# Low part of the weights first in every block of both mlp layers, and a two-column float32 product in front of each

## The chip, the cores and the metric

The kernel runs on one core of one Trainium2 chip. Its time is the device time of one execution in microseconds; of several executions the median is given. One more execution was taken with the hardware profiler, and all that is said of engines, waits and single instructions comes from that one.

The core's engines have their own instruction streams: PE (TensorE) multiplies matrices, with its weight loads listed apart as PEld; DVE (VectorE) and ACT (ScalarE) do elementwise work; POOL (GpSimd) some more of it; SP (SyncE) issues DMAs. PE writes its results to PSUM, which has eight banks of 512 float32 columns.

## The reference

A trunk of two layers over 256 tokens of width 1024, in float32. Layer 0 mixes tokens with a short gated convolution, layer 1 with a dilated window attention of 8 heads and 3 groups. After the mixer, each layer has a squared-ReLU mlp of width 4096 and a gate on a per-layer input:

```python
h = h + mixed
h = h + squared_relu_mlp(rmsnorm(h, norm_mlp[i]), mlp_w_up[i], mlp_w_down[i])
ple_gate = jax.nn.sigmoid(rmsnorm(h, norm_ple[i]) @ ple_w_gate[i])
h = h + ple_gate * (p[i] @ ple_w_proj[i])
...
def squared_relu_mlp(h, w_up, w_down):
    return jnp.square(jax.nn.relu(h @ w_up)) @ w_down
```

At the end stands one more rmsnorm.

## The kernel before

**Numbers in two parts.** The products run in the type float32r, which is a shortened float32. To keep the precision, each float32 operand is split into a high part, which is the value rounded to float32r, and a low part, which is the rest. A product of x and w is then made of three: high by high, high by low, low by high. Weights come from HBM in slabs of eight 128x128 blocks (`load_to`, on SP's queue). ACT makes the high part of a slab (L356) and DVE the low part (L295, called from `split_to`), up to LOOK slabs ahead of the block that PE works on.

**Blocks.** `block` (from L367) issues PE's work for one 128x128 block of weights. There are three kinds. Kind "n" has three products of 256 columns, one for each of the three partial products (acc_o, acc_C, acc_B, acc_g of layer 0, and the qk of the first head). Kind "w" has two: a short one, low weights by high x, 256 columns into the first half of a PSUM bank, and a long one, high weights by both parts of x side by side, 512 columns into the whole bank. Kind "t" has the weights as the moving operand (acc_v, and acc_g of layer 1). All matmuls of all kinds are issued by L392. "w" serves both mlps (acc_u for the up part, acc_d for the down part), the acc_X of the convolution (key "sc_in"), and the qk of heads 1 to 7 (key "qkv").

**Two halves.** In kind "w", blocks come in pairs: `half` 0 and `half` 1 are two neighbouring column blocks of the weights with the same x, each with a bank of its own. Two lines decide the order of the two products:

```python
products = ((dst[:, 0, :], wlo, x[0][:, k % 2, :]), (flat(dst), whi, flat(x[2][:, k % 2, :, :])))
...
products = products[::-1] if half and key != "qkv" else products
```

So, for every key but "qkv", a pair goes short, long, long, short, and the next pair begins with a short one again. For "qkv" it goes short, long, short, long.

**The order of the work.** `make_plan` writes the whole order of blocks and steps by hand: `begin`, the products of the per-layer input, the convolution, its output projection (acc_o), the mlp of layer 0, the gate, the attention head by head, its output projection (acc_o), the mlp of layer 1, and the last gate with the final norm. `mlp_plan` writes one mlp. It has the up part, 16 pairs of column blocks with 8 blocks each along the width (the first two pairs are interleaved by `head_start`, since x becomes ready bit by bit), then the down part, 4 pairs of column blocks with 32 blocks each. After the fourth pair of the up part stands a step "stat_rows", which has two PE products of its own (ssq, L500). Other steps put float32 products between the blocks: "stat" (ssq, L477: two products of the constant `ones`, two columns each), "scores" (sc, L684), "turn" (transposes, L702) and "values" (o, L723).

**Banks.** `bank` takes one of eight PSUM banks; a block opens its accumulation when its name is first met, and `close` gives it to the step that empties it. The first product of an accumulation has start set and overwrites, all others add. `sums` empties the two banks of a pair: ACT copies the second half of a bank (L411) and DVE adds the first half to it.

Of the kernel before, what the change touches and what calls it, by code (L numbers as in the profile page):

```python
# [219 lines left out]
def width(key):  # L220
    return {"v": GROUPS, "gate1": 4, "proj1": 4}.get(key, 1)
# [32 lines left out]
def tile_trunk(ctx: ExitStack, tc: tile.TileContext, plan, slabs, ap, out):  # L254
    nc = tc.nc
# [7 lines left out]
    def const(shape, name, dtype=F32):  # L263
        return cpool.tile(shape, dtype, tag=name, name=name)
# [15 lines left out]
    def bank(name):  # L280
        return psum.tile([P, 2, S], F32, tag="ps", name=name)
# [9 lines left out]
    def flat(t):  # L291
        return t.rearrange("p i s -> p (i s)")
# [6 lines left out]
    ones = const([P, P], "ones")  # L299
# [8 lines left out]
    acc, left, opened = {}, {}, set()  # L308
    for op in plan:
        if op[0] != "do":  # L310
            key = ((*op[4], op[5]), 0) if op[0] == "w" else (op[4], op[5] if op[0] == "n" else 0)
# [48 lines left out]
    def weights(item):  # L360
        si, at = place[item]
        split_to(si + min(LOOK, 1 + si // 3))
        hi, lo = parts[si]
        n = width(item[0]) * P
        return hi[:, at : at + n], lo[:, at : at + n]

    def block(kind, key, k, col, name, half, operand, m=0, cuts=1):  # L367
        name = (*name, half) if kind == "w" else name
        if name not in opened:
            acc[name] = bank("acc_" + "_".join(map(str, name)))  # L370
        left[name, half if kind == "n" else 0] -= 1
        whi, wlo = weights((key, k, col))
        x = state[operand][k // 2]
        if kind == "n":
            dst = acc[name][:, half, :]
            products = ((dst, wlo, x[0][:, k % 2, :]), (dst, whi, x[1][:, k % 2, :]), (dst, whi, x[0][:, k % 2, :]))

            products = products[::-1] if key == "proj0" else products
        elif kind == "w":

            dst = acc[name]
            products = ((dst[:, 0, :], wlo, x[0][:, k % 2, :]), (flat(dst), whi, flat(x[2][:, k % 2, :, :])))

            products = products[::-1] if half and key != "qkv" else products
        else:
            n = width(key) * P // cuts
            whi, wlo = (t[:, m * n : (m + 1) * n] for t in (whi, wlo))
            dst = flat(acc[name])[:, :n]
            xhi, xlo = (t[:, k % 2, half * P : (half + 1) * P] for t in x[:2])
            products = ((dst, xhi, whi), (dst, xhi, wlo), (dst, xlo, whi))  # L390
        for n, (to, a, b) in enumerate(products):
            nc.tensor.matmul(  # L392
                to,
                a,
                b,
                start=n == 0 and name not in opened,
                stop=n == len(products) - 1 and left[name, half if kind == "n" else 0] == 0,
                skip_group_check=True,
            )
            opened.add(name)  # L400
# [430 lines left out]
    for op in plan:  # L831
        if op[0] != "do":
            block(*op)
        elif op[1] in URGENT:
            with tc.high_priority(offset=HURRY):
                steps[op[1]](*op[2:])
        else:
            steps[op[1]](*op[2:])
# [87 lines left out]
```

## Time and profile before

| what | us |
| --- | --- |
| median of 3 executions | 781.18 |
| lowest and highest of them | 781.16, 781.47 |
| the profiled execution | 780.81 |
| its span, from the first to the last instruction | 779.0 |
| granted TensorE clock, mean over the span | 0.998 of full speed |

The span is shorter than the execution, because starting and ending the program stand outside it. Busy times of the page are unions of the times of single instructions. A matmul's time in a row (395 ns, say) is longer than the distance to the next one, because matmuls overlap in the array; the pace of PE is read from the distances of starts, or from the chain of work, which gives a run of products with its length and its count. In the names, acc_u<-x,wlo is a product with the low part of the weights, acc_u<-x,whi one with the high part. A float32 product shows as two records of PE, a float32r product as one.

### The profile page before, as it was taken

What the parts mean: (1) busy time and instruction counts of PE and PEld (TensorE: products, weight loads), DVE (VectorE), ACT (ScalarE), POOL (GpSimd) and SP (SyncE); (2) the same over time, 40 slices, a digit from 0 to 9 for tenths busy, and PEclk for the clock granted to TensorE, in tenths of its full rate; (3) what the DMA queues carried; (4) which work ended last, traced back from release to release, by engine and by line L of the source; (5) the groups of instructions that cost most, each with busy time, mean ns of one, the idle gap of its engine ahead of it and who ended that gap; (6) DMA issues with size and microseconds to landing.
All of it is one profiled execution on the core that took longest, in us unless ns stands there. A gap on an engine that the chain in (4) does not pass through costs nothing.

```text
span 779.0 us, 12527 instructions
## 1 busy us (share of the span) xinstructions
PE 770.6 (99%) x4856; PEld 701.7 (90%) x4856; DVE 574.6 (74%) x834; ACT 441.4 (57%) x679; POOL 168.0 (22%) x110
## 2 busy tenths in 40 slices
PE   9999999999999999999999999999999999999996
PEld 8999998888888899989989989989988888888885
DVE  6997779898556669888768768767698887555564
ACT  7654565565444446557655655655675555444454
POOL 0000000000000000177867867865000000000002
PEclk9999999999999999999999999999999999999999
DMA  9855555556555554654555455455465556555521
GB/s 319 291 197 189 188 187 183 194 176 201 185 192 185 194 181 142 211 184 153 157 175 163 149 175 164 150 174 190 136 194 188 186 191 190 187 190 191 188 94 55
DMA packets 42539, 140.97 MB, mean 181 GB/s; under 512 B 4848, under 2 KB 6128, under 8 KB 42480
## 3 DMA queue, kind: packets, MB, share of 16 engines
q1 hardware_dynamic: 41904, 139.61, 55.0%
q8 instruction: 38, 0.62, 0.3%
q10 hardware_dynamic: 576, 0.56, 0.2%
q14 instruction: 21, 0.17, 0.1%
HBM read 139.10 MB, written 1.05 MB: 180 GB/s over the span
## 4 chain that ended last, share of the span: by engine, by line
PE 97%; issue 1%; DVE 1%; DMA 0%; POOL 0%; ACT 0%; SPq 0%; POOLq 0%; DVEq 0%
PE acc_u L392 23%; PE acc_d L392 23%; PE acc_qk L392 17%; PE acc_v L392 9%; PE acc_o L392 6%; PE acc_g L392 5%; PE acc_C L392 3%; PE acc_B L392 3%; PE acc_X L392 3%; PE acc_p L392 1%; PE o L723 1%; PE sc L684 1%; PE tp L702 1%; PE sc L681 1%; PE o L717 1%
## 5 line engine op out<-in xcount | busy, mean ns | idle before, releaser
L295 DVE TENSOR_TENSOR wlo<-raw,whi 128x1024 fp32r<-128x1024 f32 (+2 forms) x277 | 350.6, 1272 | 159.2 <-ACT whi L356 157.3
L356 ACT ACTIVATE whi<-raw 128x1024 fp32r<-128x1024 f32 (+2 forms) x277 | 278.4, 1007 | 218.8 <-PE acc_d L392 77.1
L392 PE MATMUL acc_u<-x,whi 128*128 128x512 f32 x512 | 160.8, 395 | 0.0
L392 PE MATMUL acc_d<-u,whi 128*128 128x512 f32 x512 | 160.8, 395 | 0.0
L392 PE MATMUL acc_qk<-x,whi 128*128 128x512 f32 (+1 forms) x432 | 134.5, 368 | 0.0
L462 POOL TENSOR_TENSOR n<-v,power 128x4 f32<-128x4 f32 (+1 forms) x6 | 5.2, 862 | 518.8 <-DVE v L487 514.3
L392 PEld LDWEIGHTS acc_d<-u,wlo 128*128 128x128 f32 x512 | 96.2, 188 | 22.7
L392 PEld LDWEIGHTS acc_u<-x,wlo 128*128 128x128 f32 x512 | 96.2, 188 | 22.6
L392 PE MATMUL acc_qk<-x,wlo 128*128 128x256 f32 x384 | 107.8, 281 | 0.0
L392 PE MATMUL acc_u<-x,wlo 128*128 128x256 f32 x512 | 101.3, 278 | 0.0
L392 PE MATMUL acc_d<-u,wlo 128*128 128x256 f32 x512 | 100.9, 278 | 0.0
L392 PEld LDWEIGHTS acc_qk<-x,whi 128*128 128x128 f32 x432 | 77.9, 188 | 13.7
L651 POOL TENSOR_TENSOR rot<-qk,sinr 16x512 f32<-16x512 f32 x44 | 78.3, 1780 | 3.0
L392 PEld LDWEIGHTS acc_u<-x,whi 128*128 128x128 f32 x512 | 78.0, 189 | 0.0
L392 PEld LDWEIGHTS acc_d<-u,whi 128*128 128x128 f32 x512 | 77.9, 189 | 0.0
L392 PEld LDWEIGHTS acc_qk<-x,wlo 128*128 128x128 f32 x384 | 72.5, 189 | 0.0
L392 PE MATMUL acc_v<-whi,x 128*128 128x384 f32 x256 | 68.8, 339 | 0.0
L648 POOL TENSOR_TENSOR qk<-qk,cosr 128x512 f32<-128x512 f32 x22 | 36.8, 1671 | 53.2 <-DVE qk L412 41.9
L392 PEld LDWEIGHTS acc_v<-whi,x 128*128 128x128 f32 x256 | 46.6, 188 | 0.0
L392 PE MATMUL acc_o<-y,whi 128*128 128x256 f32 x256 | 46.4, 283 | 0.0
L657 POOL TENSOR_TENSOR qk<-qk,rot 48x512 f32<-48x512 f32 x22 | 42.9, 1948 | 1.7
L392 PE MATMUL acc_v<-wlo,x 128*128 128x384 f32 x128 | 42.9, 335 | 0.0
(174 smaller groups left out, 1038.9 us busy)
## 6 DMA issues: line engine op xcount, KB each, us to landing
raw<-in_w SPq DMA_DIRECT2D x230, 512.0 KB, 3.4
raw<-in_w SPq DMA_DIRECT2D x32, 384.0 KB, 3.1
raw<-in_w SPq DMA_DIRECT2D x10, 256.0 KB, 5.2
h<-in_xT SPq DMA_DIRECT2D x4, 256.0 KB, 5.4
mask<-in_mask SPq DMA_DIRECT2D x2, 256.0 KB, 4.2
gain<-in_gain SPq DMA_DIRECT2D x2, 256.0 KB, 4.9
out<-htg SPq DMA_DIRECT2D x2, 256.0 KB, 2.1
raw<-in_w SPq DMA_DIRECT2D x3, 128.0 KB, 3.5
```

Source lines behind the costliest of these rows:

```text
L295: nc.vector.tensor_tensor(out, a, f32(b), ALU.subtract)
L356: nc.scalar.activation(hi[:, :width], t[:, :width], AF.Copy)
L392: nc.tensor.matmul(to, a, b, start=n == 0 and name not in opened, stop=n == len(products) - 1 and left[name, half if kind == "n" else 0] == 0,
L462: nc.gpsimd.tensor_tensor(y, v, power[:, : v.shape[1]], ALU.pow)
L648: engine.tensor_tensor(t, p, both(cosr), ALU.mult)
L651: engine.tensor_tensor(r[dst : dst + 16], p[src : src + 16], sinr[src : src + 16].unsqueeze(1).to_broadcast([16, 2, S]), ALU.mult,)
L657: engine.tensor_tensor(t[:48], t[:48], r[:48], ALU.add)
L681: nc.tensor.matmul(ps[:, :S], q[:, 0, own], k[:, 1, :], start=n == 0, stop=n == 2)
L684: nc.tensor.matmul(ps[:, (g + 1) * P : (g + 2) * P], t[:, 0, own], t[:, 1, own], start=True, stop=True)
L702: nc.tensor.transpose(ps[n // 2][:, n % 2, b * P : (b + 1) * P], sm[:, n * P : (n + 1) * P], ident)
L717: nc.tensor.matmul(ps[:, 0, :], a, b[:, kb, :], start=kb == 0 and n == 0, stop=False, skip_group_check=True)
L723: nc.tensor.matmul(ps[:, 0, b * P : (b + 1) * P], v12[:, b, g * P : (g + 1) * P], t[:, g, b * P : (b + 1) * P], start=False, stop=g == 1, ...
```

## The change

In `block`, the order of the two products of a pair is reversed for the second half only with the key "sc_in". Both mlps so go short, long, short, long, as "qkv" did before. And where the accumulation ("u", 0, 0) is opened, which is the first block of each mlp, one float32 product comes first: the constant `ones`, 128x128, by two columns of it, into the first two columns of the new bank. The block's own first product has start set and overwrites what it left.

```diff
@@ -368,6 +368,9 @@
         name = (*name, half) if kind == "w" else name
         if name not in opened:
             acc[name] = bank("acc_" + "_".join(map(str, name)))
+            if name == ("u", 0, 0):
+
+                nc.tensor.matmul(flat(acc[name])[:, :2], ones, ones[:, :2], start=True, stop=True, skip_group_check=True)
         left[name, half if kind == "n" else 0] -= 1
         whi, wlo = weights((key, k, col))
         x = state[operand][k // 2]
@@ -381,7 +384,7 @@
             dst = acc[name]
             products = ((dst[:, 0, :], wlo, x[0][:, k % 2, :]), (flat(dst), whi, flat(x[2][:, k % 2, :, :])))
 
-            products = products[::-1] if half and key != "qkv" else products
+            products = products[::-1] if half and key == "sc_in" else products
         else:
             n = width(key) * P // cuts
             whi, wlo = (t[:, m * n : (m + 1) * n] for t in (whi, wlo))
```

## The prediction

> **What bounds the kernel now.** I read the page's busy shares first, then the waits of the matmul engine alone, then the chain of work that ended last in order of time.
>
> ```profile
> span 779.0 us, 12527 instructions
> ...
> PE 770.6 (99%) x4856; PEld 701.7 (90%) x4856; DVE 574.6 (74%) x834; ACT 441.4 (57%) x679; POOL 168.0 (22%) x110
> ...
> PEclk9999999999999999999999999999999999999999
> ```
>
> ```profile
> PE warm L534 <- DVE power L530: 1.0, 1, 1.0
> PE acc_p L392 <- ACT whi L356: 0.2, 1, 0.2
> ```
>
> PE is busy for 99% of the span at a granted clock in the top tenth of every slice, and the profile finds only 1.2 us in which it sat idle for another engine, all of it at the start of the kernel. So a microsecond saved or added in PE's stream of products is a microsecond of the kernel, unless an engine behind it falls late. The chain says how long each run of products takes:
>
> ```profile
> 99.94 3.72 PE acc_o L392 x31
> 103.66 22.30 PE acc_u L392 x128
> ...
> 126.19 66.89 PE acc_u L392 x384
> 193.08 89.17 PE acc_d L392 x512
> ...
> 332.89 16.64 PE acc_qk L392 x96
> ...
> 360.39 5.55 PE acc_qk L392 x32
> ...
> 369.14 11.11 PE acc_qk L392 x64
> ...
> 563.75 22.30 PE acc_u L392 x128
> ...
> 586.28 66.89 PE acc_u L392 x384
> 653.17 89.17 PE acc_d L392 x512
> ...
> 761.66 2.04 PE acc_g L392 x9
> ```
>
> The columns are start, length, what, and how many. One mlp takes 22.30 + 66.89 + 89.17 = 178.36 us for 1024 products, two take 356.72 us for 2048: 174.18 ns a product, half of them short (256 columns, low part of the weights) and half long (512 columns, high part). Three other rows give the pace of products of the same shapes. acc_o has short ones alone: 3.72 / 31 = 120.0 ns. The acc_g of the last stage has long ones alone: 2.04 / 9 = 226.7 ns. A short and a long one at their own paces would be 346.7 ns. The qk stage from 332.89 on mixes both lengths as the mlp does, but takes the short one first in every block: 16.64 / 96 = 173.33 ns, so 346.7 ns a pair, exactly the sum. The mlp has 348.4 a pair. What it loses is 1.7 ns a pair, and it is visible only because there are 1024 pairs:
>
> ```profile
> L392 PE MATMUL acc_u<-x,whi 128*128 128x512 f32 x512 | 160.8, 395 | 0.0
> L392 PE MATMUL acc_d<-u,whi 128*128 128x512 f32 x512 | 160.8, 395 | 0.0
> L392 PE MATMUL acc_u<-x,wlo 128*128 128x256 f32 x512 | 101.3, 278 | 0.0
> L392 PE MATMUL acc_d<-u,wlo 128*128 128x256 f32 x512 | 100.9, 278 | 0.0
> ```
>
> (512 short products into acc_u and 512 into acc_d, over both layers.) The order stands in the timeline of PE, first the mlp, then qk:
>
> ```profile
> 200.00 0.63 PE L392 MATMUL acc_d<-u,whi 128*128 128x512 f32 x2
> 200.47 0.39 PE L392 MATMUL acc_d<-u,wlo 128*128 128x256 f32 x2
> 200.70 0.63 PE L392 MATMUL acc_d<-u,whi 128*128 128x512 f32 x2
> 201.16 0.40 PE L392 MATMUL acc_d<-u,wlo 128*128 128x256 f32 x2
> ...
> 338.28 0.27 PE L392 MATMUL acc_qk<-x,wlo 128*128 128x256 f32 x1
> 338.39 0.40 PE L392 MATMUL acc_qk<-x,whi 128*128 128x512 f32 x1
> 338.63 0.28 PE L392 MATMUL acc_qk<-x,wlo 128*128 128x256 f32 x1
> ```
>
> In the mlp two long ones are followed by two short ones; in qk they alternate.
>
> **The change part by part.** *The order.* Both mlps become alternating. No product is added or dropped in this part. At the qk row's pace the 2048 products take 2048 x 173.33 = 354.99 us, which is 1.73 us less than 356.72. The other two qk rows bound it: 5.55 / 32 = 173.44 gives 355.20 (1.52 less), 11.11 / 64 = 173.59 gives 355.52 (1.20 less). Those two are short, so their last hundredth and the change to the next kind of work weigh more in them; I take 1.73, from the longest run, and keep 1.20 for the range. Below it I keep zero, for the case that the loss doesn't come from the order; that is a rival.
>
> Does the low part come late now? In a block of the second half it is wanted one long product earlier, some 0.23 us. But every one of the mlp's 128 slabs of eight blocks begins with a block of the first half, which takes its low part first already. So the moment at which a slab must be split doesn't move. The splits also run ahead: of all that ScalarE waits for before a high part, the largest entry is PE, giving a buffer back.
>
> ```profile
> ACT whi L356 <- PE acc_d L392: 77.1, 46, 1.7
> ```
>
> If that cover went, PE would show waits for VectorE's low part, and it has none now. PSUM: a second-half bank is opened by a short product instead of a long one, at about the same moment, and emptied after the same last block. No DMA, no queue and no wait is moved.
>
> *The float32 product.* One stands in front of the first block of each mlp, into the same bank, with nothing new to wait for (the constant of ones is from the start). The nearest rows are the two float32 products of two columns in a stat step, with the same constant, among short products:
>
> ```profile
> 319.76 0.28 PE L392 MATMUL acc_qk<-x,wlo 128*128 128x256 f32 x1
> 319.88 0.40 PE L392 MATMUL acc_qk<-x,whi 128*128 128x256 f32 x2
> 320.12 0.51 PE L477 MATMUL ssq<-ones,tot 128*128 128x2 f32 x4
> 320.49 0.36 PE L392 MATMUL acc_qk<-x,wlo 128*128 128x256 f32 x1
> 320.69 0.40 PE L392 MATMUL acc_qk<-x,whi 128*128 128x256 f32 x2
> ```
>
> Two products are four records, so one is two. From the first record to the second product behind them it is 320.69 - 320.12 = 0.57 us; the one short product in that stretch would take 0.12 (319.76 to 319.88). Four records cost 0.45 us, one float32 product 0.225, the two of the change 0.45. Note where: the records take 0.37, and the first short product behind them takes 0.20 instead of 0.12. Both mlps begin without a gap:
>
> ```profile
> 103.26 0.40 PE L392 MATMUL acc_o<-y,whi 128*128 128x256 f32 x2
> 103.50 0.28 PE L392 MATMUL acc_u<-x,wlo 128*128 128x256 f32 x1
> 103.62 0.63 PE L392 MATMUL acc_u<-x,whi 128*128 128x512 f32 x2
> ```
>
> Two short ones at 103.26 and the next at 103.50: 0.12 each, so there is no wait that could hide the product. Bounds: nothing, if it lands in a wait that I don't see; 0.90, if each costs what the two together do. I take 0.45. What it buys is not in the cost: the qk runs of 64 and 32 begin behind other work (v products, float32 scores), and all keep about the same pace, so I see no need for it in the traces.
>
> *The sum.* The profiled execution took 780.81 us, 1.81 beyond its span. 780.81 - 1.73 + 0.45 = 779.53. The median of the timed runs, 781.18, lies 0.37 above this execution, so the forecast is **779.9 us**, 1.28 us or 0.16% less. By the bounds: from 779.4 (full gain, free product) to 780.9 (781.18 - 1.20 + 0.90).
>
> **A rule against it.** In the busy shares, weight loads fill 90% of a span of which products fill 99%, so loads run beside products. The Trainium skill, page "TensorE: Matmul & The Clock Gate", section "The mechanism", says that a weight load overlaps products in flight only when it goes to another row group, and both use all rows here; the section "LDWEIGHTS (loading the stationary operand)" gives 128 columns / 1.2, an estimate of 107 ns a load. By it each load is paid in full whatever its neighbour, and order can't matter. The trace is against the rule: 120.0 ns a short product has no room for a load in line.
>
> **The rivals.** *The order is neutral.* Each product's loss belongs to its own load, bank or address, and two neighbours of a length are innocent. Then only the two float32 products are left: 781.18 + 0.45 = 781.6. For it: 1.7 ns a pair is small, and qk's weights, banks and run lengths differ from the mlp's. Against: qk's products have the same shapes, operand types and alternating banks, and its pace is the bare sum of the two lengths. This is also how it looks if the pace holds only until the next interruption (the two row-sum products in the middle of the up part) and falls back: 256 of 2048 products would gain, 0.2 us. The rule of the page above would give the same time. 13%.
>
> *The product is free.* It fits into a moment in which PE waits for its bank or for x, or it costs a small part of the stat's share: 781.18 - 1.73 = 779.45. For it: a two-column product is tiny. Against: the row of four records, and the start without a gap. 13%.
>
> *The alternation settles in a slow rhythm.* The mlp enters it from short products at 120.0, qk from others; a long one took about (200.47 - 200.00) / 2 = 0.235 us in the pair of the mlp. If the alternating stream holds both at these slower values, a pair is 120 + 235 = 355 ns, 6.6 more than 348.4, and 1024 pairs cost 6.8 us: 781.18 + 6.8 + 0.45 = 788.4. It is slower by my bound once a pair costs more than 348.4 + (1.56 - 0.45) / 1.024 = 349.5. For it: what sets the rhythm isn't shown by this trace, and the start after a float32 product is the place where a short one takes 0.20. Against: that 0.20 is seen once after each such product, not on and on, and every long qk run has the fast rhythm. 14%.
>
> **How the numbers follow.** 60% for the forecast, 13% neutral, 13% free, 14% slow. About 0.2%, 1.56 us, is what a measurement of this kernel can tell from no change: faster lies below 779.62, slower above 782.74. Faster is the free product, 13%, and a twentieth for the low end of the forecast (a product under 0.17 us at full gain): 0.18. Slower is the slow rhythm: 0.14. The rest is within: 0.68. The range goes from the free product with full gain, 779.4, to the neutral case with a little for the product's upper bound, 781.8. It leaves out the slow rhythm and little else.
>
> **What would show it.** Right: the chain's mlp rows fall to about 22.2, 66.6 and 88.7 us; PE's timeline there shows one short and one long record by turns, the first short one of each mlp takes 0.20, and two records of the new product stand ahead of it. Neutral: rows of 66.89 and 89.17 stay. Slow: a row above 67.1 for 384 products or 89.5 for 512 (349.5 a pair). Free: the step from the last acc_o to the first acc_u is as long as before. My working is wrong if PE shows idle time for VectorE's low parts, if the pace changes in the middle of the up part, or if stages whose products were not touched change their length.

## The result, and the profile after

The changed kernel takes **786.6 us** (median of 4 runs, 786.35 to 786.95) against 781.17 for the kernel before (4 runs, 781.05 to 781.47). The ratio is 1.0066, with a 95% interval of 1.0054 to 1.0078. It is 5.4 us slower where 1.3 us less was forecast. One run of a later kernel (the changed one with its row sums one block later) took 946.41 us at a granted clock of 0.752, where all the other runs had 0.997 to 0.999; the ratio given for that kernel leaves this run out.

The chain of work of the changed kernel, in order of time (start, length, what, how many; L373 is the new product, L395 the old L392):

```profile
104.27 0.12 PE acc_u L373 x2
104.39 22.71 PE acc_u L395 x128
...
127.34 67.84 PE acc_u L395 x384
195.18 90.45 PE acc_d L395 x512
...
336.27 16.64 PE acc_qk L395 x96
...
567.23 22.71 PE acc_u L395 x128
...
590.18 67.84 PE acc_u L395 x384
658.02 90.45 PE acc_d L395 x512
```

One mlp now takes 0.12 + 22.71 + 67.84 + 90.45 = 181.12 us where it took 178.36. Twice the difference is 5.5 us, all of the measured loss. A block (one short and one long product) takes 2 x 90.45 / 512 = 353.3 ns; it was 348.4. The qk row, from which the forecast took its pace, is what it was to the hundredth. The clock is no other either: 0.999 in the profiled execution, 0.998 before. And PE waits for nothing new:

```profile
PE warm L537 <- DVE power L533: 1.0, 1, 1.0
PE acc_p L395 <- ACT whi L356: 0.2, 1, 0.2
```

So the products themselves come at greater distances. PE's timeline at the start of the first mlp shows how (the first column is the start):

```profile
104.11 0.28 PE L373 MATMUL acc_u<-ones 128*128 128x2 f32 x2
104.25 0.36 PE L395 MATMUL acc_u<-x,wlo 128*128 128x256 f32 x1
104.45 0.39 PE L395 MATMUL acc_u<-x,whi 128*128 128x512 f32 x1
104.68 0.28 PE L395 MATMUL acc_u<-x,wlo 128*128 128x256 f32 x1
104.80 0.39 PE L395 MATMUL acc_u<-x,whi 128*128 128x512 f32 x1
105.03 0.28 PE L395 MATMUL acc_u<-x,wlo 128*128 128x256 f32 x1
105.15 0.40 PE L395 MATMUL acc_u<-x,whi 128*128 128x512 f32 x1
105.39 0.28 PE L395 MATMUL acc_u<-x,wlo 128*128 128x256 f32 x1
105.51 0.40 PE L395 MATMUL acc_u<-x,whi 128*128 128x512 f32 x1
105.75 0.28 PE L395 MATMUL acc_u<-x,wlo 128*128 128x256 f32 x1
```

Behind the new product the first short one takes 0.20, as forecast. Apart from that the first two blocks go at the pace of qk; from the third on, two of every three long products need 0.24 instead of 0.23. The starts in the trace are kept to the nanosecond. From them, the distances from each product to the next, block by block (short, long), in the three rhythms that matter here:

```
fast (qk behind v)              112 233 | 117 231 | 112 233 | 117 231       346.7 a block
slow (mlp, changed kernel)      113 233 | 117 241 | 120 236 | 113 233       353.3 a block
qk behind float32 scores        117 230 | 117 230 | 116 230 | 117 230       346.7 a block
```

The slow one is a cycle of three blocks, 346 + 358 + 356 = 1060 ns. I call its blocks place 1 (113, 233), place 2 (117, 241) and place 3 (120, 236). In the changed kernel it runs from the third block of each mlp to its last, with a short disturbance at the two row-sum products.

### The profile page after: what moved, and what is told of

The parts are those of the page before. It is cut to its first block, busy times and chain, and to the rows that moved or that the text cites. A ratio compares the mean times of both kernels' runs of the same rounds, so it can differ in the third digit from the quotient of the medians.

```text
span 785.2 us, 12535 instructions
## 1 busy us (share of the span) xinstructions
PE 776.6 (99%) x4860; PEld 704.9 (90%) x4860; DVE 572.5 (73%) x834; ACT 445.6 (57%) x679; POOL 168.1 (21%) x110
## 4 chain that ended last, share of the span: by engine, by line
PE 96%; DMA 1%; issue 1%; DVE 1%; ACT 0%; POOL 0%; POOLq 0%; DVEq 0%; ACTq 0%
PE acc_u L395 23%; PE acc_d L395 23%; PE acc_qk L395 17%; PE acc_v L395 8%; PE acc_o L395 6%; PE acc_g L395 4%; PE acc_C L395 3%; PE acc_B L395 3%; PE acc_X L395 3%; PE o L726 1%; PE sc L687 1%; PE tp L705 1%; PE sc L684 1%; PE o L720 1%; DMA h<-in_xT 1%
## 5 line engine op out<-in xcount | busy, mean ns | idle before, releaser
L395 PE MATMUL acc_u<-x,whi 128*128 128x512 f32 x512 | 181.1, 399 | 0.0
L395 PE MATMUL acc_d<-u,whi 128*128 128x512 f32 x512 | 181.0, 399 | 0.0
L395 PE MATMUL acc_u<-x,wlo 128*128 128x256 f32 x512 | 144.0, 281 | 0.0
L395 PE MATMUL acc_d<-u,wlo 128*128 128x256 f32 x512 | 143.8, 281 | 0.0
L395 PE MATMUL acc_qk<-x,whi 128*128 128x512 f32 (+1 forms) x432 | 134.5, 368 | 0.0
L395 PEld LDWEIGHTS acc_d<-u,whi 128*128 128x128 f32 x512 | 96.2, 188 | 24.0
L395 PEld LDWEIGHTS acc_u<-x,whi 128*128 128x128 f32 x512 | 96.2, 188 | 23.8
L395 PE MATMUL acc_qk<-x,wlo 128*128 128x256 f32 x384 | 107.8, 281 | 0.0
L395 PEld LDWEIGHTS acc_u<-x,wlo 128*128 128x128 f32 x512 | 96.7, 189 | 0.0
L395 PEld LDWEIGHTS acc_d<-u,wlo 128*128 128x128 f32 x512 | 96.7, 189 | 0.0
L395 PEld LDWEIGHTS acc_qk<-x,whi 128*128 128x128 f32 x432 | 77.9, 188 | 13.6
L395 PEld LDWEIGHTS acc_qk<-x,wlo 128*128 128x128 f32 x384 | 72.5, 189 | 0.0
L395 PE MATMUL acc_v<-whi,x 128*128 128x384 f32 x256 | 68.8, 339 | 0.0
L395 PEld LDWEIGHTS acc_v<-whi,x 128*128 128x128 f32 x256 | 46.6, 188 | 0.0
L395 PE MATMUL acc_o<-y,whi 128*128 128x256 f32 x256 | 46.4, 283 | 0.0
L414 ACT ACTIVATE r<-acc_u 128x256 f32<-128x256 f32 x64 | 23.6, 385 | 36.5 <-PE acc_u L395 36.5
```

The source lines that it names most:

```text
L395: nc.tensor.matmul(to, a, b, start=n == 0 and name not in opened, stop=n == len(products) - 1 and left[name, half if kind == "n" else 0] == 0,
L414: nc.scalar.activation(t[:, i, :], p[:, 1, :], AF.Copy)
```

## The experiments

Two theories stood at first: E, that the way in which the stream of products is entered settles its rhythm, and M, that something in the mlp makes the alternating order slow there. Each ratio below is against runs of the kernel before on the same chip.

**The order alone.** The new product's lines are taken out of the changed kernel.

```diff
-            if name == ("u", 0, 0):
-
-                nc.tensor.matmul(flat(acc[name])[:, :2], ones, ones[:, :2], start=True, stop=True, skip_group_check=True)
```

> The alternating order in both mlps without the float32 products. Theory E (the rhythm of the stream is settled by how it is entered, and the float32 product put it into the slow one): a pair at 346.7 ns as in qk, 1.7 us under the kernel before, 779.4 us. Theory M (something in the mlp itself makes the alternating order slow there, whatever stands in front): a pair at 353.3 ns, only the 0.45 us of the two products gone from the changed kernel, 786.1 us.

Measured: 780.41 us, ratio 0.999 (0.998 to 0.9999). Neither theory said this. The chain of this kernel:

```profile
103.79 22.61 PE acc_u L392 x128
126.40 0.24 PE ssq L500 x2
126.64 66.56 PE acc_u L392 x384
193.20 88.75 PE acc_d L392 x512
```

Up to the row sums ("stat_rows") a block takes 2 x 22.61 / 128 = 353.3 ns, behind them 2 x 66.56 / 384 = 346.7, to the end. The same stream of products with the same kinds of operands has both rhythms in one run; two short products of another step (ssq) stand between. So M falls, and E is not enough: the entry was slow without any float32 product. Nor is it the operands: the 512 products of a down part are the same here (88.75 us) and in the changed kernel (90.45 us), in the same order.

**The product alone.** The product's lines go into the kernel before.

> The old order (short, long, long, short) with the float32 product in front of each mlp. Theory E: the entry changes the rhythm here too, so the pair leaves 348.3 ns, either way. Theory M: the pair stays at 348.3 ns and only the products' own cost is added, 0.45 us, 781.6 us.

Measured: 781.81 us, ratio 1.0009 (0.9999 to 1.0018). The interval reaches down to no change, so the cost is read from the chain:

```profile
104.19 0.12 PE acc_u L373 x2
104.31 22.41 PE acc_u L395 x128
...
126.96 66.89 PE acc_u L395 x384
193.85 89.17 PE acc_d L395 x512
```

66.89 and 89.17 are the rows of before to the hundredth: the old order doesn't care, and theory E, by which the pair would change here too, has failed. The product costs 0.12 + (22.41 - 22.30) = 0.23 us, 0.46 for both.

**Other products in front.** Two of them (a loop around the line), and one that is 128 columns wide:

```diff
-                nc.tensor.matmul(flat(acc[name])[:, :2], ones, ones[:, :2], start=True, stop=True, skip_group_check=True)
+                for _ in (0, 1):
+                    nc.tensor.matmul(flat(acc[name])[:, :2], ones, ones[:, :2], start=True, stop=True, skip_group_check=True)
```

```diff
-                nc.tensor.matmul(flat(acc[name])[:, :2], ones, ones[:, :2], start=True, stop=True, skip_group_check=True)
+                nc.tensor.matmul(flat(acc[name])[:, :P], ones, ones, start=True, stop=True, skip_group_check=True)
```

> The changed kernel with two float32 products of two columns in front of each mlp in place of one. Theory E: if the place within a cycle at the entry decides, the rhythm may be another than with one product: 346.7 ns a pair and about 780.3 us, or again 353.3. Theory M: 353.3 ns a pair, 0.45 us more than the changed kernel, 787.0 us.

> The changed kernel with the float32 product made 128 columns wide, as the last product of scores in front of the qk runs is. Theory E: the entry is then that of the qk runs, 346.7 ns a pair and about 780 us. Theory M: 353.3 ns a pair, 786.7 us.

Measured: 787.14 us (ratio 1.0077, 1.0061 to 1.0092) and 786.94 us (1.0073, 1.0057 to 1.009). Both are slow to the end of both mlps. That is what M expected, but M had fallen with the first run. E's forecast for the wide product, that the mlp would then be entered as the qk runs are, failed: behind the scores the first distances in qk are 200 235 | 117 230 or 201 233 | 117 235 and the runs are fast, here they are 203 229 | 117 234 | 117 241 and the mlp is slow. What decides between such entries isn't shown. What all these kernels have in common shows in the distances around the row sums of the first mlp (S: a row-sum product):

```
changed          113 233 | 117 241 | 120 231 | S 118 | S 113 | 120 233 | 117 241 | 120 236
two products     114 232 | 118 240 | 120 231 | S 119 | S 113 | 119 233 | 118 241 | 120 236
128 columns      113 233 | 117 241 | 120 231 | S 118 | S 113 | 120 233 | 117 240 | 121 236
order alone      117 241 | 120 236 | 113 233 | S 118 | S 118 | 118 231 | 112 233 | 117 231
```

The first three meet the row sums behind place 3 and come out slow; the order alone meets them behind place 1 and comes out fast. In the order alone the cycle begins with the first block of the mlp, so the 64th, the last ahead of the row sums, is at place 1. In the changed kernel place 2 first comes with the third block, one block later, and the 64th is at place 3. That gives theory R: the slow rhythm keeps itself up; the row sums end it only at place 1; the product shifted the cycle by one block and so made them miss. Its rival P: the float32 product itself makes the rhythm slow for good, and the row sums can't end it.

**The place of the row sums.** In the changed kernel they are moved one block later; in the kernel with the order alone, two (`(4, 0, 1)` in the line below, in place of `(4, 0, 0)`).

```diff
             for i in (0, 1):
                 plan.append(("w", up, k, 2 * j + i, ("u", j), i, x))
+                if (j, k, i) == (4, 0, 0):
+                    plan.append(("do", "stat_rows", 3 * layer + 1))
         plan.append(("do", "up_out", j))
-        if j == 3:
-            plan.append(("do", "stat_rows", 3 * layer + 1))
```

> The changed kernel, float32 products included, with the row-sum step of each mlp one block later (behind the 65th block instead of the 64th). Theory R (the slow rhythm is a cycle of three blocks that keeps itself up; the row sums end it only behind the block whose two products take 113 and 233 ns; the float32 product shifted the cycle by one block and so made the row sums miss): behind the row sums 346.7 ns a block until the end of the mlp, like the kernel with the order alone plus the 0.45 us of the products, 780.9 us. Theory P (the float32 product leaves PE in a slow state that the row sums don't end): 353.3 ns a block throughout, 786.6 us.

> The alternating order without the float32 products, the row sums two blocks later (behind the 66th block), where the slow cycle stands as it stood in the changed kernel (120 and 236). Theory R: they miss, 353.3 ns a block throughout both mlps, 786.1 us, though there is no float32 product. Theory P: 346.7 ns behind the row sums as in the kernel with the order alone, 780.4 us.

Measured: 781.17 us (781.05 without the run of 946.41; ratio 1.0003, 0.9993 to 1.0014) and 785.0 us (1.0049, 1.0033 to 1.0066). The chain of the changed kernel with the row sums one block later:

```profile
103.68 0.12 PE acc_u L373 x2
103.80 23.07 PE acc_u L395 x130
...
127.10 66.22 PE acc_u L395 x382
193.32 88.75 PE acc_d L395 x512
```

And of the order alone with the row sums two blocks later:

```profile
103.58 23.32 PE acc_u L392 x132
...
127.13 67.13 PE acc_u L392 x380
194.26 90.46 PE acc_d L392 x512
```

66.22 / 382 is 173.4 ns a product, fast, with the float32 product in front; 67.13 / 380 is 176.7, slow, without it. Both as R said, and neither as P said. A step of two short products, moved by one block, takes some 5.5 us out of the changed kernel (5.9 by the two chains). The runs of these two kernels scatter more than the others. Two of the first lie at 783.47 and 784.0, the other seven between 780.38 and 781.3; two of the second lie at 783.94 and 784.1, the other two at 785.89 and 786.7. One run of each was profiled, 780.38 and 785.89, and both its mlps agree with R. Whether a mlp of the runs in between took the other rhythm isn't shown.

**Another way in.** Without the products, the first block of each mlp long first; and, in another kernel, the first pair of blocks of each mlp in the old order (short, long, long, short).

```diff
-            products = products[::-1] if half and key == "sc_in" else products
+            products = products[::-1] if (half and key == "sc_in") or (name == ("u", 0, 0) and k == 0) else products
```

```diff
-            products = products[::-1] if half and key == "sc_in" else products
+            products = products[::-1] if (half and key == "sc_in") or (name == ("u", 0, 1) and k == 0) else products
```

> The alternating order without the float32 products, the very first block of each mlp long first (long, short, short, long, short, long ...). Theory R says that the entry sets the cycle, not to which side: either 346.7 ns a block from the start and 779.5 us, or the slow cycle with another phase, 780.4 us if the row sums then end it and 786.1 us if not. Theory P: the slow stretch in front of the row sums and the fast one behind them don't change, 780.4 us.

> The alternating order without the float32 products, the first pair of blocks of each mlp in the old order (short, long, long, short, then short, long ...). As in the run before: theory R 779.5 us if it enters the fast rhythm at once, else 780.4 or 786.1 by the phase at the row sums; theory P 780.4 us.

Measured: 786.37 us (ratio 1.0065, 1.0048 to 1.0081) and 785.56 us (1.0056, 1.0041 to 1.0071). Long first enters the slow cycle, meets the row sums behind place 3 and stays slow. The old-order pair enters the fast rhythm at once, and the row sums turn it slow:

```profile
103.85 22.20 PE acc_u L392 x128
...
126.28 67.84 PE acc_u L392 x384
194.12 90.45 PE acc_d L392 x512
```

22.20 / 128 is 173.4 ns in front of them, 67.84 / 384 is 176.7 behind. The step that ends the slow rhythm at place 1 turns the fast one slow here.

**Fast to the end.** Two kernels try to get past the row sums: with the first pair in the old order and the row sums one block later (the diff above), or with the row sums in their old place and an old-order pair behind them too:

```diff
-            products = products[::-1] if half and key == "sc_in" else products
+            products = products[::-1] if half and (key == "sc_in" or name in (("u", 0, 1), ("u", 4, 1)) and k == 0) else products
```

> No float32 products; alternating order, first pair of each mlp in the old order (which entered the fast rhythm at once), and the row sums one block later than before, behind the other block of the fast rhythm's two. Theory R: they put the stream into the slow rhythm behind one of the two blocks only; then 346.7 ns a block in both mlps to the end, 1.7 us under the kernel before, 779.5 us. If they do so behind either block: slow from there as with the rows in their old place, 785.6 us.

> No float32 products; alternating order, row sums in their old place, the first pair of each mlp and the first pair behind the row sums in the old order (short, long, long, short). Theory R, with the old-order pair as the thing that ends the slow cycle: 346.7 ns a block in front of and behind the row sums, 779.5 us. If the old-order pair only worked because of what stood in front of it at the start: slow behind the row sums, 785.6 us.

Measured: 785.31 us (ratio 1.005, 1.0038 to 1.0063) and **779.68 us** (ratio 0.9979, 0.9971 to 0.9988; 11 runs). The first shows that the row sums turn the fast rhythm slow behind either of its two blocks. The second is fast in both mlps to the end, and its interval lies clear of the kernel before and of the changed one. Its chain:

```profile
103.98 22.20 PE acc_u L392 x128
...
126.41 66.57 PE acc_u L392 x384
192.97 88.75 PE acc_d L392 x512
```

22.20 + 66.57 + 88.75 = 177.52 us for a mlp, 0.84 under the kernel before, 1.7 for both. That is the gain forecast for the order.

**Is an old-order pair a cure anywhere?** The first pair of blocks of every pair of column blocks is put in the old order, once in the changed kernel and once without the products.

```diff
-            products = products[::-1] if half and key == "sc_in" else products
+            products = products[::-1] if half and (key == "sc_in" or name[0] in "ud" and k == 0) else products
```

> The changed kernel, float32 products included, with the first pair of blocks of every pair of column blocks (16 in the up part, 4 in the down part of each mlp) in the old order. They stand at all places of the slow cycle. If one old-order pair ends the slow rhythm wherever it stands: 346.7 ns a block nearly throughout, 0.45 us for the products and about 0.01 us for each of the 40 pairs, 780.3 us. If it does so at some places only: slow stretches stay, between 781 and 786 us.

> The same without the float32 products. If an old-order pair ends the slow rhythm anywhere: 779.8 us. If at some places only: between 780 and 786 us. Theory P, by which only the float32 product makes the stream slow for good, gives no slow stretch behind the row sums here, 779.8 us too.

Measured: 786.7 us (ratio 1.0067, 1.0051 to 1.0082) and 786.09 us (1.006, 1.0048 to 1.0073). My expectation failed: both lie above even the 786 us that I gave as the most for a cure at some places only. The kernel without products:

```profile
127.42 67.66 PE acc_u L392 x384
195.08 90.43 PE acc_d L392 x512
```

Such a pair ended nothing within the slow rhythm, and within the fast one it started the slow: behind the row sums the old-order pair and 14 more blocks are fast or nearly so, and the next old-order pair turns them (112 233 230 114 | 119 233 | 118 241 | 120 235). Behind the float32 product it didn't help either: the changed kernel's first blocks here are 202 232 231 117 | 120 234 | 117 241.

But the pairs did not stand at all places of the slow cycle, as I had assumed. In both kernels each one within the slow rhythm begins at place 3 (117 241 | 120 236 227 113 | 119 234 | 117 241), since a pair leads to place 1 and the 14, 26 or 62 blocks up to the next pair end at place 2 each time. Pairs at places 1 and 2 were not tried. The row sums stood behind place 2 in both, with an old-order pair right behind them, and the stream came out fast (117 233 | S 117 | S 113 | 120 233 236 116 | 112 233 | 117 231). Whether row sums alone would end the slow rhythm at place 2 was not run, so R's "only at place 1" is shown against place 3 alone. In every mlp that an old-order pair led into the fast rhythm, short products alone stood right in front of it (acc_o or the row sums); that they are the reason isn't shown.

**Can qk be slow?** It was left open whether qk was fast because of its operands or because nothing disturbed it. In the kernel before, one pair in the middle of each qk run is put in the old order:

```diff
-            products = products[::-1] if half and key != "qkv" else products
+            products = products[::-1] if half and (key != "qkv" or k == 4) else products
```

> The kernel before (mlps in the old order), with one pair of blocks in the middle of every qk run of heads 1 to 7 (the fifth of eight) in the order short, long, long, short. Theory R (the two rhythms belong to the alternating order, wherever it runs; an old-order pair in the middle of the fast one turned it slow in the mlps): behind that pair the qk runs show the slow cycle, 353.3 ns a block, until v, scores or transposes end it; of 336 qk blocks about half, so some 0.7 to 1.5 us, 782.0 to 782.7 us. Theory Q (qk has something that keeps it fast, its weights, banks or operands): 346.7 ns a block again behind the pair, 781.3 us.

Measured: 782.1 us, ratio 1.0009 (0.9999 to 1.0018); the difference of the medians is 0.7 us, and the interval reaches down to no change, so it is the trace that decides. PE's timeline, from the pair on:

```profile
336.31 0.63 PE L392 MATMUL acc_qk<-x,whi 128*128 128x512 f32 x2
336.77 0.40 PE L392 MATMUL acc_qk<-x,wlo 128*128 128x256 f32 x2
337.00 0.40 PE L392 MATMUL acc_qk<-x,whi 128*128 128x512 f32 x1
337.24 0.28 PE L392 MATMUL acc_qk<-x,wlo 128*128 128x256 f32 x1
337.36 0.40 PE L392 MATMUL acc_qk<-x,whi 128*128 128x512 f32 x1
337.60 0.28 PE L392 MATMUL acc_qk<-x,wlo 128*128 128x256 f32 x1
337.72 0.40 PE L392 MATMUL acc_qk<-x,whi 128*128 128x512 f32 x1
337.95 0.28 PE L392 MATMUL acc_qk<-x,wlo 128*128 128x256 f32 x1
```

The long ones take 0.24, 0.24, 0.23 by turns: the slow cycle, in qk. In head 1 it goes on through the runs of the other two groups, through two more such pairs. Behind the scores of the later heads the rhythm of (117, 230) stands in front of the pair, and there the pair leads into (112, 233 | 117, 231), fast still; the next one turns that slow. So nothing in qk's operands keeps it fast, though the rhythm of (117, 230) outlasts one such pair.

## Why the prediction was wrong

- **What bounds the kernel: right.** PE's stream is the time. In every run that changes the mlps their rows account for the change of the whole, within the spread of its runs.
- **The order: wrong, and this is the step that failed.** "At the qk row's pace the 2048 products take 354.99 us" treated a pace as a property of the order. They took 362.00 us in the changed kernel (22.71 + 67.84 + 90.45, twice), because the pace is a property of the order and of what went before. The alternating order has a fast rhythm and a slow one, each of which keeps itself up for hundreds of products. The qk runs showed me only the fast one: they are entered behind v and float32 scores, and nothing stands within them. That the second matters is shown (an old-order pair within them turned them slow); why those entries are fast isn't. The mlps are entered behind acc_o, from which the order alone went into the slow one. The size of the gain was right where the fast rhythm held: 1.7 us.
- **The float32 product's cost: right.** 0.225 us was forecast for one; the run with the product alone shows 0.23.
- **"I see no need for it in the traces": wrong in kind.** I weighed it by its cost alone. Its real effect is to shift the slow cycle by one block against the row sums, which then no longer end it. With it the kernel takes 786.6 us, without it 780.41: 6.2 us, of which its own two uses are 0.46.
- **The slabs, banks and splits: right.** PE shows the same two waits as before. (The 128 slabs are those of both mlps, 64 for each.)
- **The slow rhythm as a rival: near the truth, at too low a chance.** I gave it 14% and 788.4 us, with every block at 355 ns. The blocks take 346, 358 and 356 ns by turns, 353.3 in the mean, and the result is 786.6. That it needs the row sums to miss it was not in it. My argument against it, that the 0.20 us behind a float32 product comes once and not on and on, looked at the wrong thing: the first distance passes, the rhythm stays. "Every long qk run has the fast rhythm" was two kinds of entry, v and scores, counted many times, and neither is that of the mlps.
- **The sentence "or if the pace changes in the middle of the up part"**, listed as a sign that the working is wrong, is what the run with the order alone shows.

The Trainium skill, page "TensorE: Matmul & The Clock Gate", section "Back-to-back issue gap", says that in a stream of loads and products both set the distance; its formula, for an isolated product at full clock, is N / 2.4 + 2.5 ns for N columns. By the formula a block would take 109 + 216 = 325 ns, an estimate. Neither has the order in it, and no run here is at 325. The same two products at the same granted clock (0.997 to 0.999) take 346.7, 348.4 or 353.3 ns a block here, by their order and by what ran before them.

What stays open is what carries the rhythm from one block to the next. The profile shows loads and products, not what lies between them, and the loads of the down parts look nearly alike: in the changed kernel each begins 2 to 5 ns behind the start of the product in front and its record is 187 to 190 ns long, in the kernel of 779.68 us 2 to 4 ns and 187 to 188 ns. That the rhythm survives hundreds of products, and that the place in the cycle at which the row sums come decides, is shown by moving them; why place 1 is a way out and place 3 isn't stays open.

## What to carry to other kernels

A pace read from one stretch of a dense product stream may be taken over to another only if the same work stands in front of it and in it; where the rows differ by a few per cent at the same shapes, look at the distances of starts over a dozen products for a cycle before you believe a mean. If a reordering of products costs or gains some tenths of a per cent, move a neighbouring step by one block and measure again, since its place may be worth more than the order. A cheap product that "does nothing" can do a lot to the products behind it.

## What the runs showed of the hardware

- Alternating products of 256 and 512 columns run at 346.7 or at 353.3 ns a block, with the same operands, and stay there: in the changed kernel the slow cycle lasts for the 512 products of a down part, and the fast one does so in the kernel with the order alone.
- Two short products behind place 1 of the slow cycle end it (113 233 | S | S), behind place 3 they don't (120 231 | S | S), and the same two start it behind either block of the fast rhythm.
- The order short, long, long, short kept 348.4 ns a block, with the float32 product in front and without it.
- A float32 product of two columns costs 0.23 us in front of float32r products: by the chain 0.12 for its two records and 0.11 as delay of what stands behind.
